# Pinning the weight-block sums of the feed-forward's second product to their place in program order

## The chip, the core and the metric

The kernel runs on one core of a Trainium2 chip. The metric is the device time of one execution in microseconds. The engines are TensorE (PE; its weight loads are PEld), VectorE (DVE), ScalarE (ACT), GpSimd (POOL) and SyncE (SP), which issues nearly all DMAs. Each works through its own queue in order; semaphores join them.

## The reference, cut to what matters

A decoder block on 512 positions of width 2048, in float32. Every product is made as three passes of a split number (high and low part), so a slice of weights costs a ScalarE copy and a VectorE subtraction before TensorE can use it.

```python
h = rmsnorm(x, norm_mix_g)
z = h @ w_in                                   # q, k, v, forget gates, zu, zv
attn = forgetting_attention(q, k, v, log_f)    # 8 heads, causal, softmax
gm = chunked_spatial_gating(zu, zv, ...)       # gelu, layernorm, 128 x 128 mixing
x = x + concat(rmsnorm(attn), rmsnorm(gm)) @ w_out
h2 = rmsnorm(x, norm_ffn_g)
a = relu(h2 @ w_ff1)                           # 2048 -> 8192
x = x + (a * a) @ w_ff2                        # 8192 -> 2048
out = rmsnorm(x, norm_final_g)
```

## The kernel before, in words

*Units and slices.* All products up to `w_ff1` are a list of units: `v0`, `qk0`, `qk1`, `v1`, `qk2`, `qk3`, `zv0`, `zv1`, `zu0`, `zu1` (16 weight slices each), eight units of the output projection (`oa`, `og`, 8 slices each) and `f0` to `f15`, the first feed-forward product (16 each): 160 + 64 + 256 = 480 slices. `run_units` walks them. For each slice it prepares the one three ahead (`load_pair`, L171, brings two slices in one DMA into one of four `raw` buffers; `split_w` makes `wh` on ScalarE, L162 or L158, and `wl` on VectorE, L163 or L159; there are four buffers of each), then issues 12 matmuls (L150 to L152), then at a unit's end its evacuation (`qk_done`, L335 and L338, for q and k), and then calls `tick()`.

*Tasks.* `tick()` advances every running task whose count of slices has run down; what a task issues then stands in program order at that slice. Attention is such a task: `head_task` issues the scores of one query block per slice (`pS`, one PSUM tile that all query blocks share), their maxima on VectorE (L380, L382), the exponential (L389), transposes (`pT`, L397), and the split of these (`ptl`, L400). So are the norms (`rB`, L146) and the gating (`u`, L532; its 128 x 128 weights `ws` come by GpSimd's queue, and L478 splits them).

*The sums.* The second feed-forward product uses seven block products instead of eight, which need sums of blocks of `w_ff2`. `sums_task` (L648) makes them ahead of time, in 64 rounds: load three blocks b12, b11, b22 (L655), two slices later add b12 to b11 and to b22 on VectorE (L657, L658), two slices later store both sums to DRAM (`t1d`, `t3d`, L660, L661), and three slices later the next round. `b_pool` has one buffer for each of the three. It starts 18 slices in. The second product (`second_product`, matmuls at L959) loads `t1d` and `t3d` again; it begins after the last slice.

*What sets the order.* Only TensorE's order is written by hand (`manual_schedule(engines={PE})`). On the other engines a scheduler orders the instructions when the kernel is built, by the time at which it takes each to be ready; an instruction whose inputs are early can so stand far ahead of its place in the program.

Of the kernel before, what the change touches and what calls it, by code (L numbers as in the profile page):

```python
# [12 lines left out]
ALU = mybir.AluOpType  # L13
# [21 lines left out]
def hybrid_block(ctx, tc, xT, win, wf_in, wout, w1, w2, cols_in, ln_in, ws_in, out):  # L35
    nc = tc.nc
# [608 lines left out]
    t1d = [dram.tile([2, P, 1024], F32, name=f"t1d{u}") for u in range(NU)]  # L645
    t3d = [dram.tile([2, P, 1024], F32, name=f"t3d{u}") for u in range(NU)]

    def sums_task():  # L648
        for u in range(NU):
            for n in range(2):  # L650
                for e in range(2):
                    c = slice(512 * e, 512 * (e + 1))
                    b11, b12, b22 = (b_pool.tile([P, 512], F32, tag=f"b{i}", name=f"b{u}{n}{e}{i}") for i in range(3))
                    for b, i in ((b12, 2), (b11, 0), (b22, 3)):
                        nc.sync.dma_start(out=b, in_=w2[8 * u + 4 * n + i][:, c])  # L655
                    yield 2
                    nc.vector.tensor_tensor(b11, b11, b12, ALU.add)  # L657
                    nc.vector.tensor_tensor(b22, b22, b12, ALU.add)  # L658
                    yield 2
                    nc.sync.dma_start(out=t1d[u][n][:, c], in_=b11)  # L660
                    nc.sync.dma_start(out=t3d[u][n][:, c], in_=b22)  # L661
                    yield 3

    mid = {}
# [355 lines left out]
    for u in range(NU):  # L1020
        f1_unit(u)
    start_task(attention_task())
    start_task(sums_task(), 18)
    run_units()
    for _ in mid["second"]:
# [51 lines left out]
```

## Time and profile before

| | us |
|---|---|
| median of 3 runs (2092.02 to 2095.45) | 2093.39 |
| the profiled execution | 2093.68 |
| its span, first to last instruction | 2090.8 |
| TensorE busy | 2029.5 (97%) |
| VectorE busy | 1268.1 (61%) |
| ScalarE busy | 903.3 (43%) |
| GpSimd busy | 225.6 (11%) |

By stage: to about 600 us run the ten units of the input projection with attention and gating beside them; to 727 us the output projection; to 1456 us the first feed-forward product; to 2053 us the second; then the last norm and the store. "Busy" counts the time in which an engine has at least one instruction under way. A wait is written "engine, line, waited for", with the total, the number of times and the longest; "[5.46 <-DMA b]" behind an instruction is the time that its engine stood idle before it, and what ended that.

### The profile page before, as it was taken

What the parts mean: (1) busy time and instruction counts of PE and PEld (TensorE: products, weight loads), DVE (VectorE), ACT (ScalarE), POOL (GpSimd) and SP (SyncE); (2) the same over time, 40 slices, a digit from 0 to 9 for tenths busy, and PEclk for the clock granted to TensorE, in tenths of its full rate; (3) what the DMA queues carried; (4) which work ended last, traced back from release to release, by engine and by line L of the source; (5) the groups of instructions that cost most, each with busy time, mean ns of one, the idle gap of its engine ahead of it and who ended that gap; (6) DMA issues with size and microseconds to landing.
All of it is one profiled execution on the core that took longest, in us unless ns stands there. A gap on an engine that the chain in (4) does not pass through costs nothing.

```text
span 2090.8 us, 24810 instructions
## 1 busy us (share of the span) xinstructions
PE 2029.5 (97%) x8992; PEld 1661.7 (79%) x8992; DVE 1268.1 (61%) x1769; ACT 903.3 (43%) x1424; POOL 225.6 (11%) x179
## 2 busy tenths in 40 slices
PE   9998998899999999999999999999999999999997
PEld 6777776778778888888888888888888888888886
DVE  7566566558676463344333443334767777777787
ACT  6233333435534243344333443335544444444455
POOL 4000001000042421121111211112000000000000
PEclk9999999999999999999999999999999999999999
DMA  6676676775763336545544455446777566666652
GB/s 238 226 241 225 224 242 214 225 230 172 229 205 112 120 121 222 221 171 199 199 166 171 171 201 200 163 171 262 270 283 262 188 245 252 215 228 241 240 203 81
DMA packets 152906, 431.13 MB, mean 206 GB/s; under 512 B 16080, under 2 KB 28496, under 8 KB 152656
## 3 DMA queue, kind: packets, MB, share of 16 engines
q1 hardware_dynamic: 152096, 427.69, 58.3%
q8 instruction: 70, 1.15, 0.2%
q10 hardware_dynamic: 432, 1.35, 0.2%
q0 software_dynamic: 256, 0.52, 0.1%
q14 instruction: 52, 0.43, 0.1%
HBM read 328.83 MB, written 100.66 MB: 205 GB/s over the span
## 4 chain that ended last, share of the span: by engine, by line
PE 72%; DMA 15%; DVE 8%; issue 3%; ACT 1%; SPq 0%; POOL 0%; DVEq 0%; POOLq 0%; ACTq 0%
PE bX L959 16%; PE ps_f L150 11%; PE ps_f L152 11%; PE ps_f L151 11%; DMA b<-in_w_dram 10%; PE bZ L959 8%; PE bY L959 4%; DMA t1d<-b 2%; DMA t3d<-b 2%; DVE b L658 1%; PE ps_og L152 1%; PE ps_og L151 1%; PE ps_og L150 1%; PE ps_oa L152 1%; PE ps_oa L150 1%
## 5 line engine op out<-in xcount | busy, mean ns | idle before, releaser
L159 DVE TENSOR_TENSOR wl_f<-raw_f,wh_f 128x512 fp32r<-128x512 f32 x256 | 193.7, 757 | 368.5 <-ACT wh_f L158 313.7
L150 PE MATMUL ps_f<-xh,wh_f 128*128 128x512 f32 x1024 | 398.9, 390 | 0.0
L152 PE MATMUL ps_f<-xh,wl_f 128*128 128x512 f32 x1024 | 398.5, 389 | 0.0
L151 PE MATMUL ps_f<-xl,wh_f 128*128 128x512 f32 x1024 | 398.4, 389 | 0.0
L787 DVE TENSOR_TENSOR wl<-raw,wh 128x1024 fp32r<-128x1024 f32 x224 | 273.8, 1227 | 135.4 <-ACT wh L786 133.6
L786 ACT CAST wh<-raw 128x1024 fp32r<-128x1024 f32 x224 | 236.2, 1054 | 262.5 <-PE bX L959 133.2
L959 PE MATMUL bX<-wh,fac 128*128 128x512 f32 x1008 | 319.9, 391 | 0.0
L158 ACT CAST wh_f<-raw_f 128x512 fp32r<-128x512 f32 x256 | 159.4, 623 | 330.9 <-PE ps_f L151 321.6
L959 PEld LDWEIGHTS bX<-wh,fac 128*128 128x128 f32 x1008 | 189.2, 188 | 46.9 <-ACT k L809 7.5
L152 PEld LDWEIGHTS ps_f<-xh,wl_f 128*128 128x128 f32 x1024 | 192.2, 188 | 40.0
L151 PEld LDWEIGHTS ps_f<-xl,wh_f 128*128 128x128 f32 x1024 | 192.2, 188 | 39.8
L150 PEld LDWEIGHTS ps_f<-xh,wh_f 128*128 128x128 f32 x1024 | 192.2, 188 | 39.8
L959 PE MATMUL bX<-wl,fac 128*128 128x512 f32 x504 | 196.3, 390 | 0.0
L959 PE MATMUL bZ<-wh,fac 128*128 128x512 f32 x512 | 162.8, 389 | 0.0
L657 DVE TENSOR_TENSOR b<-b,b 128x512 f32<-128x512 f32 x64 | 47.9, 749 | 131.6 <-DMA b<-in_w_dram 131.4
L959 PEld LDWEIGHTS bZ<-wh,fac 128*128 128x128 f32 x512 | 96.1, 188 | 19.9
L150 PE MATMUL ps_qk<-xh,wh_qk 128*128 128x512 f32 x256 | 103.7, 405 | 6.0 <-DVE qkt L335 5.7
L959 PEld LDWEIGHTS bX<-wl,fac 128*128 128x128 f32 x504 | 94.6, 188 | 18.7
L152 PE MATMUL ps_qk<-xh,wl_qk 128*128 128x512 f32 x256 | 101.2, 395 | 0.0
L151 PE MATMUL ps_qk<-xl,wh_qk 128*128 128x512 f32 x256 | 101.1, 395 | 0.0
L959 PE MATMUL bZ<-wl,fac 128*128 128x512 f32 x256 | 99.6, 389 | 0.0
L162 ACT ACTIVATE wh_qk<-raw_qk,cols 128x512 fp32r<-128x512 f32 x64 | 46.1, 722 | 87.9 <-PE ps_qk L151 64.2
(277 smaller groups left out, 3328.1 us busy)
## 6 DMA issues: line engine op xcount, KB each, us to landing
raw_f<-in_w_dram SPq DMA_DIRECT2D x128, 512.0 KB, 3.3
fac<-fc SPq DMA_DIRECT2D x112, 512.0 KB, 3.4
fac<-fac SPq DMA_DIRECT2D x112, 512.0 KB, 6.0
b<-in_w_dram SPq DMA_DIRECT2D x192, 256.0 KB, 4.3
raw<-in_w_dram SPq DMA_DIRECT2D x96, 512.0 KB, 5.0
raw_qk<-in_win_dram SPq DMA_DIRECT2D x32, 512.0 KB, 4.3
t1d<-b SPq DMA_DIRECT2D x64, 256.0 KB, 2.5
t3d<-b SPq DMA_DIRECT2D x64, 256.0 KB, 2.5
```

Of the source, the lines that this page charges most:

```text
L150: nc.tensor.matmul(ps, lhsT=ah, rhs=bh, start=start, stop=False)
L151: nc.tensor.matmul(ps, lhsT=ah, rhs=bl, start=False, stop=False)
L152: nc.tensor.matmul(ps, lhsT=al, rhs=bh, start=False, stop=stop)
L158: nc.scalar.copy(wh, raw)
L159: nc.vector.tensor_tensor(wl, raw, f(wh), ALU.subtract)
L162: nc.scalar.activation(wh, raw, AF.Copy, scale=g)
L657: nc.vector.tensor_tensor(b11, b11, b12, ALU.add)
L658: nc.vector.tensor_tensor(b22, b22, b12, ALU.add)
L786: nc.scalar.copy(wh, s)
L787: nc.vector.tensor_tensor(wl, s, f(wh), ALU.subtract)
L959: nc.tensor.matmul(banks[chain][t], lhsT=l, rhs=r, start=start and w == 0, stop=stop and w == 2, skip_group_check=True)
```

## The change

The three loads, two additions and two stores of each round are wrapped in `keep_in_program_order`. It ties an instruction behind the last one that was issued on its engine before it in program order, so the scheduler can't move it ahead of that one. It adds no instruction and no wait on a semaphore; other instructions may still move ahead of the tied ones.

```diff
+    here = tc.keep_in_program_order
+
     def sums_task():
...
                     for b, i in ((b12, 2), (b11, 0), (b22, 3)):
-                        nc.sync.dma_start(out=b, in_=w2[8 * u + 4 * n + i][:, c])
+                        here(nc.sync.dma_start(out=b, in_=w2[8 * u + 4 * n + i][:, c]))
                     yield 2
-                    nc.vector.tensor_tensor(b11, b11, b12, ALU.add)
-                    nc.vector.tensor_tensor(b22, b22, b12, ALU.add)
+                    here(nc.vector.tensor_tensor(b11, b11, b12, ALU.add))
+                    here(nc.vector.tensor_tensor(b22, b22, b12, ALU.add))
                     yield 2
-                    nc.sync.dma_start(out=t1d[u][n][:, c], in_=b11)
-                    nc.sync.dma_start(out=t3d[u][n][:, c], in_=b22)
+                    here(nc.sync.dma_start(out=t1d[u][n][:, c], in_=b11))
+                    here(nc.sync.dma_start(out=t3d[u][n][:, c], in_=b22))
                     yield 3
```

Two lines are inserted above, so behind L647 every line of the changed kernel counts two more: the loads are L657, the sums L659 and L660, the stores L662 and L663. TensorE's and GpSimd's orders are the same in both. Three places of the others, first before, then after:

VectorE in the first 100 us, between the splits of `qk` slices 3 and 4; `vl` is the evacuation of `v0`, `zf`, `dup` belong to the forget gates, `rB` is the norm row that they wait for, `b` are the sums. Before:

```order
L256 SCALAR_TENSOR_TENSOR vl_616<-ps_v_3_267,r_161,vh_615 128x512
L163 SCALAR_TENSOR_TENSOR wl_qk_3_667<-raw_qk_2_597,cols,wh_qk_3_666 128x512
L657 TENSOR_TENSOR b_1216<-b_1216,b_1217 128x512
L658 TENSOR_TENSOR b_1218<-b_1218,b_1217 128x512
L291 COPY zf<-pz 128x512
L296 COPY dup<-ident 64x8 x2
L297 TENSOR_TENSOR dup<-dup,ident 64x8 x2
L657 TENSOR_TENSOR b_1445<-b_1445,b_1446 128x512
L146 COPY rB<-pb_mix 128x512
```

After, with the rows that follow:

```order
L256 SCALAR_TENSOR_TENSOR vl_616<-ps_v_3_267,r_161,vh_615 128x512
L163 SCALAR_TENSOR_TENSOR wl_qk_3_667<-raw_qk_2_597,cols,wh_qk_3_666 128x512
L291 COPY zf<-pz 128x512
L296 COPY dup<-ident 64x8 x2
L297 TENSOR_TENSOR dup<-dup,ident 64x8 x2
L146 COPY rB<-pb_mix 128x512
L163 SCALAR_TENSOR_TENSOR wl_qk_4_693<-raw_qk_4_690,cols,wh_qk_4_692 128x512
L163 SCALAR_TENSOR_TENSOR wl_qk_5_715<-raw_qk_4_690,cols,wh_qk_5_714 128x512
L163 SCALAR_TENSOR_TENSOR wl_qk_6_753<-raw_qk_6_750,cols,wh_qk_6_752 128x512
L302 TENSOR_TENSOR z<-pz_730,rB 128x512
L659 TENSOR_TENSOR b_708<-b_708,b_709 128x512
```

The sums of the fourth and fifth round stood there (with three rounds ahead of them); now none stands ahead of `rB`, and the first sum of all follows slice 6.

SP's queue at the same place of the program, at the weight loads (`raw_qk`) of slices 12 and 14 of `qk0` and of the next unit; `b` are the blocks, `t1d` and `t3d` the stores. Before:

```order
L655 DMA b_1446<-in_w_dram 128x512
L655 DMA b_1445<-in_w_dram 128x512
L655 DMA b_1447<-in_w_dram 128x512
L660 DMA t1d_194<-b_1445 128x512
L661 DMA t3d_210<-b_1447 128x512
L655 DMA b_1680<-in_w_dram 128x512
L171 DMA raw_qk_12_868<-in_win_dram 128x1024
L655 DMA b_1679<-in_w_dram 128x512
L655 DMA b_1681<-in_w_dram 128x512
L660 DMA t1d_194<-b_1679 128x512
L661 DMA t3d_210<-b_1681 128x512
L171 DMA raw_qk_14_904<-in_win_dram 128x1024
```

After:

```order
L171 DMA raw_qk_12_868<-in_win_dram 128x1024
L662 DMA t1d_193<-b_708 128x512
L663 DMA t3d_209<-b_710 128x512
L657 DMA b_863<-in_w_dram 128x512
L657 DMA b_862<-in_w_dram 128x512
L171 DMA raw_qk_14_904<-in_win_dram 128x1024
L657 DMA b_864<-in_w_dram 128x512
L171 DMA raw_qk_0_940<-in_win_dram 128x1024
L171 DMA raw_qk_2_974<-in_win_dram 128x1024
L171 DMA raw_qk_4_1036<-in_win_dram 128x1024
L662 DMA t1d_193<-b_862 128x512
L663 DMA t3d_209<-b_864 128x512
```

A round of five transfers stood at nearly every weight load; now four weight loads lie between the stores of the first round and those of the second.

VectorE inside the first feed-forward product, at the splits of slices 10 to 15 of one `f` unit. Before:

```order
L159 TENSOR_TENSOR wl_f_10_6685<-raw_f_10_6682,wh_f_10_6684 128x512
L159 TENSOR_TENSOR wl_f_11_6701<-raw_f_10_6682,wh_f_11_6700 128x512
L159 TENSOR_TENSOR wl_f_12_6725<-raw_f_12_6722,wh_f_12_6724 128x512
L159 TENSOR_TENSOR wl_f_13_6741<-raw_f_12_6722,wh_f_13_6740 128x512
L159 TENSOR_TENSOR wl_f_14_6761<-raw_f_14_6758,wh_f_14_6760 128x512
L159 TENSOR_TENSOR wl_f_15_6777<-raw_f_14_6758,wh_f_15_6776 128x512
```

After:

```order
L159 TENSOR_TENSOR wl_f_10_6685<-raw_f_10_6682,wh_f_10_6684 128x512
L159 TENSOR_TENSOR wl_f_11_6701<-raw_f_10_6682,wh_f_11_6700 128x512
L159 TENSOR_TENSOR wl_f_12_6725<-raw_f_12_6722,wh_f_12_6724 128x512
L159 TENSOR_TENSOR wl_f_13_6741<-raw_f_12_6722,wh_f_13_6740 128x512
L659 TENSOR_TENSOR b_6716<-b_6716,b_6717 128x512
L660 TENSOR_TENSOR b_6718<-b_6718,b_6717 128x512
L159 TENSOR_TENSOR wl_f_14_6761<-raw_f_14_6758,wh_f_14_6760 128x512
L159 TENSOR_TENSOR wl_f_15_6777<-raw_f_14_6758,wh_f_15_6776 128x512
```

No sum stood in this product before; now a pair stands in every seven slices of it.

## Rows read from the trace of the kernel before

**Rows 1.** Stages: length, busy (instructions) PE, PEld, DVE, ACT, POOL; clock, DMA share, GB/s.

```profile
30.00:110.00 80.00, 74.11 (x312) 58.07 (x311) 45.15 (x70) 28.63 (x44) 10.76 (x9) 0.96 0.66 215
110.00:600.00 490.00, 448.62 (x2011) 365.31 (x2009) 321.45 (x679) 192.09 (x359) 38.70 (x39) 0.98 0.69 223
727.30:1455.70 728.40, 728.32 (x3232) 602.81 (x3231) 312.86 (x397) 299.12 (x519) 100.88 (x69) 1.00 0.51 187
1515.80:1568.10 52.30, 52.30 (x230) 42.87 (x230) 36.44 (x36) 24.81 (x28) 0.00 (x0) 1.00 0.77 283
```

**Rows 2.** TensorE's waits, 30 to 605 us: total, times, longest.

```profile
PE pS L150 <- DVE mx L382: 19.2, 11, 3.5
PE pm L150 <- DVE u L532: 6.1, 3, 3.2
PE ps_qk L150 <- DVE qkt L335: 5.7, 2, 3.6
PE ps_zv L151 <- DVE wl_zv L163: 4.9, 1, 4.9
PE pT L397 <- DVE ptl L400: 4.7, 4, 1.7
PE pz L300 <- DVE rB L146: 4.1, 1, 4.1
```

**Rows 3.** VectorE's waits, 30 to 605 us.

```profile
DVE b L657 <- DMA b<-in_w_dram: 131.4, 44, 5.7
DVE b L658 <- DMA b<-in_w_dram: 20.6, 20, 2.1
DVE rs L390 <- ACT p L389: 13.0, 18, 1.0
```

**Rows 4.** The timeline at 75 us: start, duration, instruction, idle before it.

```profile
75.43 0.69 DVE L657 TENSOR_TENSOR b<-b,b 128x512 f32<-128x512 f32 x1 [5.46 <-DMA b<-in_w_dram]
76.04 0.68 DVE L146 COPY rB<-pb_mix 128x512 f32<-128x512 f32 x1
...
76.87 1.19 PE L300 MATMUL pz<-zf,dup 128*128 128x512 f32 x1 [4.06 <-DVE rB L146]
```

**Rows 5.** The page, part 4: the chain that ended last, by line.

```profile
PE bX L959 16%; PE ps_f L150 11%; PE ps_f L152 11%; PE ps_f L151 11%; DMA b<-in_w_dram 10%; PE bZ L959 8%; PE bY L959 4%; DMA t1d<-b 2%; DMA t3d<-b 2%; DVE b L658 1%; PE ps_og L152 1%; PE ps_og L151 1%; PE ps_og L150 1%; PE ps_oa L152 1%; PE ps_oa L150 1%
```

**Rows 6.** Short stretches, columns as in rows 1; the clock is third from last.

```profile
75.10:81.90 6.80, 5.03 (x10) 3.38 (x11) 5.40 (x9) 0.00 (x0) 0.00 (x0) 0.50 0.55 154
121.20:124.60 3.40, 3.39 (x15) 2.83 (x16) 3.37 (x6) 2.89 (x5) 0.00 (x0) 1.00 0.96 311
228.70:232.10 3.40, 3.40 (x10) 2.63 (x9) 2.53 (x9) 1.47 (x4) 0.00 (x0) 0.50 1.00 255
...
587.00:590.40 3.40, 3.28 (x8) 2.64 (x9) 2.88 (x7) 0.30 (x1) 0.00 (x0) 0.51 0.87 278
```

**Rows 7.** The chain in order of time: start, length, what; 24 dense matmuls.

```profile
1461.15 5.44 PE bY L959 x24
```

**Rows 8.** DMA issues by line: count, KB each, median us from issue to landing.

```profile
raw_f<-in_w_dram SPq DMA_DIRECT2D x128, 512.0 KB, 3.3
...
b<-in_w_dram SPq DMA_DIRECT2D x192, 256.0 KB, 4.3
...
t1d<-b SPq DMA_DIRECT2D x64, 256.0 KB, 2.5
```

**Rows 9.** The timeline at 364 us.

```profile
363.73 0.80 DVE L478 TENSOR_TENSOR wsl<-ws,wsh 128x128 fp32r<-128x128 f32 x1 [4.59 <-ACT wsh L477]
...
364.95 0.45 PE L150 MATMUL pS<-qkh 128*128 128x384 f32 x1 [3.51 <-DVE mx L382]
```

**Rows 10.** The page, part 5: the two splits of a slice; busy, mean ns of one.

```profile
L159 DVE TENSOR_TENSOR wl_f<-raw_f,wh_f 128x512 fp32r<-128x512 f32 x256 | 193.7, 757 | 368.5 <-ACT wh_f L158 313.7
...
L158 ACT CAST wh_f<-raw_f 128x512 fp32r<-128x512 f32 x256 | 159.4, 623 | 330.9 <-PE ps_f L151 321.6
```

**Rows 11.** Waits of all engines, 620 to 1455 us.

```profile
ACT wh_f L158 <- PE ps_f L151: 321.6, 171, 2.9
```

## The prediction

> **What bounds the kernel now.** I read the busy time by stage first. From 727 us on TensorE is busy for 728.32 of 728.40 us, so nothing that only moves work can shorten that stretch. Between 30 and 600 us it is busy for 74.11 of 80 us and 448.62 of 490 us, 47.3 us short, and the granted clock is 0.96 and 0.98 there instead of 1.00 [rows 1]. So all that can be won stands in the first 600 us.
>
> Next come TensorE's waits in that stretch. They add up to the same 47.3 us, and nearly every one ends on VectorE: softmax maxima (19.2 us), the gating product (6.1), the evacuation of q and k (5.7), a weight split (4.9), transposes (4.7), the norm row rB (4.1), and five smaller ones, 2.6 together [rows 2].
>
> Then, what VectorE itself was doing. It stood 131.4 + 20.6 = 152 us at the two weight-block sums, waiting for their blocks to land, up to 5.7 us at a time; every other wait is small beside it: 13.0 us in 18 pieces for the exponentials, none over 1.0 [rows 3]. One place shows the link. VectorE reaches L657 and idles 5.46 us for a block; right behind it in its queue stands the copy of rB, which needs nothing from that block; TensorE waits 4.06 us for rB [rows 4]. An engine that works in order and meets a sum whose data is still travelling holds up everything behind it. In the chain that ended last, the loads of b are 10% and the stores 2% + 2% of the span [rows 5]: the sums run one after the other through a single set of buffers, and for 600 us that loop leads the kernel.
>
> **What the gaps cost in clock.** Seven stretches have the granted clock at 0.50, each beginning at one of these gaps. Six are 3.4 us long and hold 10, 10, 10, 8, 9 and 8 matmuls, 55 in all, where an undisturbed 3.4 us holds 15 [rows 6]. That is 90 - 55 = 35 matmuls, at 5.44/24 = 0.227 us each [rows 7], 7.9 us. The seventh, 75.1 to 81.9 us, holds 10 where 30 fit: 20 x 0.227 = 4.5 us, of which 6.80 - 5.03 = 1.8 us is idle time already counted, so 2.8 us. Together 10.7 us. The whole loss before 600 us is 47.3 + 10.7 = 58.0 us.
>
> The Trainium skill (TensorE: Matmul & The Clock Gate, What's actually happening) says that the slow level is the resting state and that activity releases it. The traced gaps agree only partly: after the 3.6 us wait for the evacuation of q and k [rows 2], at 121 us, the clock stayed at 1.00 [rows 6], so I count the seven stretches seen, not one per gap.
>
> The skill (Perfetto Trace Analysis, Identifying the Most-Contended Engine) also holds matmul busy time a poor measure and wants the busy share of weight loads instead. By that share, 0.726 and 0.746 early against 0.828 where TensorE is dense [rows 1], the loss would be 80 x 0.102/0.828 + 490 x 0.082/0.828 = 58 us; taken over the whole span it would promise 17% in the dense stretch too, which its 0.227 us from one matmul to the next denies.
>
> **What the change does, part by part.** No arithmetic, byte or instruction is added; TensorE's and GpSimd's order stay as they were. What moves is 128 sums on VectorE and 320 transfers on SP's queue.
>
> *Sums on VectorE.* The task starts after 18 weight slices and has one round per 7 slices, 64 rounds; with 12 matmuls a slice takes 12 x 0.227 = 2.72 us when dense, so a round comes every 19 us instead of every 9. The order shows it: no sum stands before rB any more, and later one pair stands in every seven slices. In the order 29 rounds stay ahead of the feed-forward product and 35 fall into it, the dense stretch. A round's loads are issued right behind the stores of the round before, some five slices (13 us) ahead of its sums, against 4.3 us to landing [rows 8]; so the waits of 152 us should all but vanish, and the rounds that stay cost their own 2 x 0.69 us [rows 4].
>
> *What stays of the 58.0 us.* First, a gap that the sums don't make: at 365 us TensorE waits 3.51 us for a maximum, after VectorE stood 4.59 us at a gating weight [rows 9], which comes by GpSimd's queue; that weight keeps its place among its neighbours. It stays with its slow stretch: 3.5 + 5 x 0.227 = 4.6 us. Second, the five small waits, 2.6 us. Third, the rounds left on VectorE. Of 64 first sums 44 waited for a block [rows 3], so 20 didn't; I put the gaps beside those 20 at about 3 us, an estimate of the size of the five small waits in [rows 2], 0.15 us each; 29 rounds then cost 4.4 us. Fourth, one further slow stretch, 1.3 us (35/6 x 0.227). Sum: 4.6 + 2.6 + 4.4 + 1.3 = 12.9 us.
>
> *The dense stretch.* It takes up 35 rounds: 35 x 1.38 = 48 us of VectorE, busy there for 313 of 728 us. What hides it: the splits of a slice start as soon as one of four buffers comes free, three slices (8.2 us) before use, and take 0.62 + 0.76 us [rows 10], so 6.8 us are to spare against 1.38; ScalarE waits there for TensorE, 321.6 us in all, and TensorE for nobody [rows 1, 11]. If that cover were gone it would cost up to 48 us. DMA: a round moves five times 256 KB, 1.31 MB; 35 in 728 us add 63 GB/s to 187, 250 in all, and the second product runs at 283 GB/s with TensorE full [rows 1]. I take nothing, and 48 us as the far end.
>
> *SP's queue.* A store waits for its sum, and in order behind it stand the next blocks (which wait for the store to land, 2.5 us [rows 8]) and three or four weight loads. After the first stores the next weight load is for slice 14 of its unit, while the sums stand beside slice 6: eight slices, 21.8 us; the closest I find in the dense stretch is six, 16.3 us. Against that stand 1.4 us of sums, 2.5 of landing and 3.3 for the weights [rows 8]: 7.2 us. I take nothing here either.
>
> **Sum.** The profiled execution took 2093.68 us, 2.9 us more than its span; the median of the three runs is 2093.39, so I use the first as it is. 2093.7 - 58.0 + 12.9 = 2048.6, said as 2049.
>
> **Rivals.** *The attention chain holds the gaps itself.* Matrix products of scores come 2.72 us apart and share one PSUM tile; if softmax on VectorE is too slow for that without any sum in between, the 19.2 + 4.7 us of waits on maxima and transposes stay [rows 2], with their three slow stretches, 17 matmuls short, 3.9 us. Won would be 58.0 - 23.9 - 3.9 = 30.2, less the small 2.6 and about half of the rounds' 4.4: 25 us, giving 2069. Against it: VectorE is busy for 321 of 490 us there, sums included, and its own waits in that chain are 1 us or less [rows 3].
>
> *Slower: SP's queue starves the weights.* Pinned stores stand before weight loads in the dense stretch, where no slack was needed so far. If a store comes so late that the load behind it misses its slice, a round costs a landing, 3.3 us [rows 8]; 35 rounds make 116 us, less the 45 won: 2164. It decides the sign from 45/35 = 1.3 us per round on. Against it: the 16.3 against 7.2 us above; the order would have to slip by three slices. The Trainium skill (Perfetto Trace Analysis, DMA Optimizations) speaks on its side: it suggests one DMA-capable engine for inputs and another for outputs, and here both share SP, before and after; no row shows a weight split late for its load in the dense stretch.
>
> *Little happens.* The pins hold the order but the early gain is given back in the dense stretch, 1.3 us a round, or the gaps have causes that the sums only accompany: 2093. The 4.06 us behind one block speak against it.
>
> **How the numbers follow.** Forecast 0.74, held by attention 0.17, starved weights 0.05, little 0.04. The forecast's own ends are 2036 (everything won, 2093.7 - 58.0) and about 2056 (the 12.9 that stays half as much again); the second rival reaches to 2069. The range 2035 to 2070 holds both. Within 0.2% (4 us) a measurement here can't tell from no change. Faster by more: 0.74 + 0.17, 0.91; same 0.03; slower 0.06, most of it starved weights.
>
> **What would show it.** Right: VectorE's wait for b under 10 us in all; TensorE's idle time before 600 us at some 12 us, the largest piece the gating weight's; at most two stretches at half clock there; sums spread to about 1,350 us; TensorE still full, at some 250 GB/s, from the first feed-forward product on. Wrong: waits on maxima as long as before with no sum beside them (the first rival), or TensorE waiting for splits after 700 us, with SP's loads held by stores (the second).

## The result, and the profile after

The changed kernel took 2031.43 us, the median of 4 runs (2029.58 to 2031.70), beside 2094.01 for the kernel before (4 runs, 2092.02 to 2095.45): a ratio of 0.970, interval 0.9683 to 0.9717. A second set of runs gave 2031.11, ratio 0.9697 (0.968 to 0.9715). The forecast was 2049 with a range from 2035 to 2070. Its sign and its mechanism hold; the time lies 4 us below the range, so the gain was put too small, 45 us for 62. The rest of this part reads the profiled execution of 2031.65 us, whose span is 2029.9.

First the stages, as in [rows 1]: length, busy time of PE, PEld, DVE, ACT and POOL with their instructions, then clock, DMA share and GB/s. The stages start earlier now; 675 us is where 727 was. The first matmul of `f0` itself starts at 755.4 us in the kernel before, not at 727 as the list of stages has it, and at 694.7 us in the changed one, so both stretches open with the end of the output projection. The last row is one short stretch, read below.

```profile
30.00:110.00 80.00, 78.97 (x349) 64.11 (x348) 43.52 (x67) 32.69 (x50) 10.76 (x9) 1.00 0.38 128
110.00:575.00 465.00, 462.01 (x2139) 383.69 (x2139) 296.28 (x635) 202.42 (x377) 52.34 (x50) 1.00 0.45 149
575.00:675.00 100.00, 100.00 (x458) 82.72 (x457) 72.30 (x81) 41.20 (x64) 37.53 (x24) 1.00 0.52 174
675.00:1396.00 721.00, 720.92 (x3200) 596.79 (x3199) 349.69 (x461) 295.25 (x514) 101.17 (x70) 1.00 0.71 253
329.70:333.10 3.40, 3.40 (x10) 2.83 (x9) 2.28 (x10) 1.40 (x4) 1.29 (x3) 0.50 0.09 28
```

TensorE now lacks 1.0 us of the first 80 and 3.0 of the next 465, and the clock is at full speed in both. The dense stretch has taken the other rounds (253 GB/s for 187) and TensorE is still busy for all of it. VectorE works no less: 349.69 of 721 us there, where [rows 1] had 313 of 728.

TensorE's waits between 30 and 605 us, all of them (total, times, longest), where [rows 2] had 47.3 us:

```profile
PE pS L150 <- DVE mx L382: 3.0, 1, 3.0
PE ps_v L151 <- DVE wl_v L163: 0.8, 1, 0.8
PE ps_v L150 <- ACT wh_v L162: 0.2, 1, 0.2
```

Next, the view of the tile `b`. Its rows give minimum, median and maximum of one operation in ns and its first and last start; the last two lines are the idle time ahead of the sums, with its count:

```profile
L659 DVE TENSOR_TENSOR b<-b,b x64: 673/686/1809, 73.0 to 1341.6; 128x512 f32<-128x512 f32 x64
...
its engine sat idle before it (us, times) until:
  DMA b<-in_w_dram: 1.5, 2
```

The 152 us of VectorE's waits for blocks [rows 3] are 1.5 us, and a sum still takes 0.69 us. Before, the same view has the first sums from 40.2 to 609.8 us, one round every 569.6/63 = 9.0 us; now it is one every 1268.6/63 = 20.1 us.

The one gap left is the gating weight's, 35 us earlier than in [rows 9] and smaller. The timeline at 328 us (start, duration, instruction, idle before it and what ended that):

```profile
328.19 0.80 DVE L478 TENSOR_TENSOR wsl<-ws,wsh 128x128 fp32r<-128x128 f32 x1 [1.48 <-ACT wsh L477]
...
329.41 0.41 PE L150 MATMUL pS<-qkh 128*128 128x384 f32 x1 [2.99 <-DVE mx L382]
```

Right behind it lies the only stretch at half clock (1.2 instead of 2.4 GHz), the last row of the stages: 10 matmuls in 3.40 us where 15 fit, as in [rows 6].

The page's chain that ended last, by engine and by line, where [rows 5] had the loads of `b` at 10%:

```profile
PE 96%; DVE 2%; issue 1%; DMA 1%; ACT 0%; POOL 0%; SPq 0%; POOLq 0%; DVEq 0%
PE bX L961 17%; PE ps_f L150 11%; PE ps_f L152 11%; PE ps_f L151 11%; PE bZ L961 8%; PE bY L961 4%; PE ps_qk L150 3%; PE ps_qk L152 3%; PE ps_qk L151 3%; PE ps_oa L152 1%; PE ps_oa L150 1%; PE ps_zu L152 1%; PE ps_oa L151 1%; PE ps_zu L151 1%; PE ps_zu L150 1%; PE ps_zv L150 1%
```

No transfer of `b` is left in that line; the chain is TensorE's own work. The transfers themselves became slower, not faster, as the last number (median us to landing) shows beside [rows 8]:

```profile
raw_f<-in_w_dram SPq DMA_DIRECT2D x128, 512.0 KB, 4.8
...
b<-in_w_dram SPq DMA_DIRECT2D x192, 256.0 KB, 4.5
t1d<-b SPq DMA_DIRECT2D x64, 256.0 KB, 3.1
```

It costs TensorE nothing, though ScalarE now waits a little for weights, which it didn't before. From 620 to 1395 us:

```profile
ACT wh_f L158 <- DMA raw_f<-in_w_dram: 15.3, 5, 4.3
```

### The profile page after: what moved, and what is told of

The parts are those of the page before. It is cut to its first block, busy times and chain, and to the rows that moved or that the text cites. A ratio compares the mean times of both kernels' runs of the same rounds, so it can differ in the third digit from the quotient of the medians.

```text
span 2029.9 us, 24801 instructions
## 1 busy us (share of the span) xinstructions
PE 2011.3 (99%) x8992; PEld 1656.5 (82%) x8992; DVE 1273.8 (63%) x1769; ACT 904.1 (45%) x1424; POOL 226.3 (11%) x179
## 4 chain that ended last, share of the span: by engine, by line
PE 96%; DVE 2%; issue 1%; DMA 1%; ACT 0%; POOL 0%; SPq 0%; POOLq 0%; DVEq 0%
PE bX L961 17%; PE ps_f L150 11%; PE ps_f L152 11%; PE ps_f L151 11%; PE bZ L961 8%; PE bY L961 4%; PE ps_qk L150 3%; PE ps_qk L152 3%; PE ps_qk L151 3%; PE ps_oa L152 1%; PE ps_oa L150 1%; PE ps_zu L152 1%; PE ps_oa L151 1%; PE ps_zu L151 1%; PE ps_zu L150 1%; PE ps_zv L150 1%
## 5 line engine op out<-in xcount | busy, mean ns | idle before, releaser
L158 ACT CAST wh_f<-raw_f 128x512 fp32r<-128x512 f32 x256 | 159.3, 623 | 319.2 <-PE ps_f L151 285.8
L163 DVE SCALAR_TENSOR_TENSOR wl_qk<-raw_qk,cols,wh_qk 128x512 fp32r<-128x512 f32 x64 | 47.8, 749 | 64.1 <-ACT wh_qk L162 63.7
```

What stands on the lines that cost most here:

```text
L158: nc.scalar.copy(wh, raw)
L163: nc.vector.scalar_tensor_tensor(wl, raw, g, f(wh), ALU.mult, ALU.subtract)
```

## The experiments

The theory: VectorE, working in order, stood at sums whose blocks were still travelling, and TensorE waited for what stood behind them. The rivals: it was the DMA traffic of the early rounds, or the sums' own 1.4 us a round, or attention. All times are medians; edits are shown against the changed kernel, and none leaves any of the computation out.

### Which of the pins does it

Only the two sums pinned, loads and stores left to the scheduler:

```diff
-                        here(nc.sync.dma_start(out=b, in_=w2[8 * u + 4 * n + i][:, c]))
+                        nc.sync.dma_start(out=b, in_=w2[8 * u + 4 * n + i][:, c])
...
-                    here(nc.sync.dma_start(out=t1d[u][n][:, c], in_=b11))
-                    here(nc.sync.dma_start(out=t3d[u][n][:, c], in_=b22))
+                    nc.sync.dma_start(out=t1d[u][n][:, c], in_=b11)
+                    nc.sync.dma_start(out=t3d[u][n][:, c], in_=b22)
```

> Only the two sums of a round are pinned; loads and stores float as before the change. Waiting theory (VectorE no longer meets a sum whose block still travels): the sums stand where they stand in the changed kernel, so the whole gain stays: 2031 us, within 3 us; VectorE's wait for b under 5 us. If SP's order makes the gain, most of it goes: 2060 us or more.

2032.28 us, ratio 0.9697 (0.9676 to 0.9718): the whole gain. The sums run from 72.5 to 1341.4 us and VectorE waits 1.5 us for blocks, as in the changed kernel. The 128 pins on VectorE are enough; a store can't go ahead of its sum, nor a load ahead of the store that frees its buffer, so the transfers follow.

The other half, only the transfers pinned:

```diff
-                    here(nc.vector.tensor_tensor(b11, b11, b12, ALU.add))
-                    here(nc.vector.tensor_tensor(b22, b22, b12, ALU.add))
+                    nc.vector.tensor_tensor(b11, b11, b12, ALU.add)
+                    nc.vector.tensor_tensor(b22, b22, b12, ALU.add)
```

> Only loads and stores are pinned; the sums float, and in the order they stand up to seven slices ahead of their place in the changed kernel. Waiting theory: where the order takes a block to have landed sooner than it does, VectorE waits again; some 20 to 60 us of waits for b in all, 2033 to 2050 us. If SP's order makes the gain: 2031 us and no waits.

2034.44 us, 0.9706 (0.9682 to 0.9731): nearly all of it again. Either half holds the pace; the scheduler, left free with the sums, only puts them a little too early. VectorE's waits at the first sum of a pair, from 30 to 605 us and from 675 to 1395:

```profile
DVE b L659 <- DMA b<-in_w_dram: 27.6, 16, 4.2
```

```profile
DVE b L659 <- DMA b<-in_w_dram: 73.8, 32, 5.7
```

And its dense stretch, columns as in the stages above:

```profile
675.00:1396.00 721.00, 719.95 (x3195) 595.70 (x3194) 347.62 (x456) 295.09 (x513) 101.22 (x69) 1.00 0.71 250
```

Here is a point that the theory in its short form misses. VectorE stands for 73.8 us at sums and TensorE loses 1 us. A stall at a sum is a loss only where what stands behind it is wanted at once; in the dense stretch splits are made some slices ahead. Early on, 27.6 us in 16 waits left TensorE's waits between 30 and 1395 us at 5.3 us in all. The many waits of before, 152 us with a round every 9 us, did use up the slack.

### Was it the traffic?

Traffic without waits put back into the first 600 us: 128 copies of 256 KB from DRAM to DRAM, on SP's queue.

```diff
+    spare = [dram.tile([P, 512], F32, name=f"spare{i}") for i in range(4)]
+
+    def traffic_task():
+        for r in range(64):
+            for j in range(2):
+                here(nc.sync.dma_start(out=spare[2 * (r % 2) + j], in_=w2[2 * r + j][:, 0:512]))
+            yield 3
...
+    start_task(traffic_task(), 12)
```

> The changed kernel with 128 copies of 256 KB from DRAM to DRAM, two in every three slices over the first 200 slices, pinned on SP's queue: about 33 MB, so that the first 600 us move about as much as before the change (223 GB/s against 149). Nothing waits for them, no sum moves. Waiting theory: 2031 to 2035 us. Traffic theory (weights and blocks land sooner because less is moved beside them): half of the gain or more is lost, 2060 us or more.

2034.90 us, 0.9709 (0.9677 to 0.9741). Its stage from 110 to 575 us:

```profile
110.00:575.00 465.00, 459.94 (x2125) 381.89 (x2124) 295.04 (x634) 201.74 (x376) 52.36 (x50) 0.99 0.60 202
```

At 202 GB/s, against 223 before [rows 1] and 149 after the change, TensorE lacks 5.1 us of 465, and all of it is one wait, the gating weight's, which grew from 3.0 to 5.1 us. So 53 of the 74 GB/s came back, as copies that stay in DRAM, for 3.5 us by the medians or 1.9 by the ratios, whose intervals overlap. The traffic isn't what held TensorE.

### Putting the waits back

The loads of a round issued at the sums' own slice, on ScalarE's queue:

```diff
                     for b, i in ((b12, 2), (b11, 0), (b22, 3)):
-                        here(nc.sync.dma_start(out=b, in_=w2[8 * u + 4 * n + i][:, c]))
-                    yield 2
+                        here(nc.scalar.dma_start(out=b, in_=w2[8 * u + 4 * n + i][:, c]))
...
-                    yield 3
+                    yield 5
```

> The changed kernel with the three loads of a round issued by ScalarE's queue and the sums pinned at the same slice as the loads, one round per seven slices as in the changed kernel: the sums' place and the traffic are those of the changed kernel, but VectorE meets each sum before its blocks have landed, some 4 us each. Waiting theory: about 27 early rounds x 4 us = 100 us of waits, of which TensorE takes over about a third with its slow clock, 2055 to 2080 us; from the first feed-forward product on the 6.8 us to spare hide them. Traffic theory, and the theory that VectorE just has less to add early: 2031 us.

2036.81 us, 0.9718 (0.9684 to 0.9752). As a test of the early waits this failed: the pin ties a sum to what stands before it, but other instructions may still go ahead of it, and the scheduler let them. Early on only 6.4 + 4.7 us of waits came back. In the dense stretch 46.0 + 45.1 us did, and TensorE was busy there for 720.89 of 721 us. That second part says the same as the experiment before: in the dense stretch such waits are covered.

So the pace was changed instead, everything left pinned on SP and VectorE. Four slices a round, then three, then two:

```diff
-                    yield 2
+                    yield 1
                     here(nc.vector.tensor_tensor(b11, b11, b12, ALU.add))
                     here(nc.vector.tensor_tensor(b22, b22, b12, ALU.add))
                     yield 2
...
-                    yield 3
+                    yield 1
```

> The changed kernel with a round per four slices instead of seven (sums one slice after the loads, next loads one slice after the stores): 43 rounds in the first 600 us instead of 25, still pinned. A round needs some 9 us, four slices give 11 to 13. Waiting theory: no waits for b to speak of, 2031 to 2036 us. Load theory (VectorE and the DMA queues just have less to do early): 43 of 62 rounds are back where they were, so (43 - 25)/(62 - 25), about half of the gain, is lost: 2060 us.

2030.01 us, 0.9694 (0.9666 to 0.9722). The sums now end at 823 us, 12.0 us a round, and 50 of the 64 rounds have their first sum before 675 us (28 in the changed kernel), at 194 GB/s from 110 to 575 us; TensorE waits 2.4 us between 30 and 605 us, less than in the changed kernel. Rounds that don't wait cost the early part nothing that can be seen.

```diff
-                    yield 2
+                    yield 1
...
-                    yield 2
+                    yield 1
...
-                    yield 3
+                    yield 1
```

> A round per three slices, pinned: 57 rounds in the first 600 us, nearly as many as before the change (62), with the same traffic and the same additions. Three slices give 8.2 us where dense and 9.8 with attention beside them, against 9 for a round. Waiting theory: waits return where slices are dense, 20 to 60 us in all, 2033 to 2055 us. Load theory: nearly all of the gain is lost, 2085 us.

2044.61 us, 0.9764 (0.9736 to 0.9792). VectorE's waits, 30 to 700 us:

```profile
DVE b L659 <- DMA b<-in_w_dram: 45.0, 23, 4.7
...
DVE b L660 <- DMA b<-in_w_dram: 9.9, 12, 2.0
```

The waits are back, TensorE lacks 670 - 658.34 = 11.7 us of that stretch (its waits in the changed kernel were 4.0), and the time is 13.2 us above the changed kernel's.

```diff
-                    yield 2
+                    yield 1
...
-                    yield 2
+                    yield 1
...
-                    yield 3
```

> A round per two slices, pinned: faster than its own loop of load, sum and store can turn. In the order the 64 rounds stand between slices 21 and 159. Waiting theory: the loop leads the kernel, 64 rounds x 9 us = 576 us for 138 slices that take 450 us by themselves: 2130 to 2170 us, slower than before the change, with over 150 us of VectorE waits for b. Load theory: as before the change, 2090 us.

2113.03 us, 1.0091 (1.0061 to 1.012): 0.9% slower than before, with every instruction of the rounds pinned, though less so than the 2130 to 2170 that I had put down. VectorE's waits from 30 to 700 us, and the stage that lost most:

```profile
DVE b L659 <- DMA b<-in_w_dram: 127.6, 58, 5.7
DVE b L660 <- DMA b<-in_w_dram: 31.9, 33, 4.9
```

```profile
110.00:575.00 465.00, 404.56 (x1773) 325.07 (x1774) 289.74 (x637) 167.20 (x314) 27.79 (x31) 0.96 0.72 234
```

So much for the pins as such. The place that the program gives to a round has to leave it the time for its loop, and the pin then holds it there.

### A stall of VectorE with no sum and no transfer

To see what a stall alone does, one copy in attention (`nFm`, once per head) is made nine times over, eight of them for nothing:

```diff
-        nc.vector.tensor_tensor(nFm.rearrange("p (t c) -> p t c", c=P), pB.rearrange("p (t c) -> p t c", c=P),
-                                mask.unsqueeze(1).broadcast_to([P, NT, P]), ALU.add)
+        for _ in range(9):
+            tc.keep_in_program_order(nc.vector.tensor_tensor(
+                nFm.rearrange("p (t c) -> p t c", c=P), pB.rearrange("p (t c) -> p t c", c=P),
+                mask.unsqueeze(1).broadcast_to([P, NT, P]), ALU.add))
```

> The changed kernel with the row of masked gates nFm computed nine times instead of once for each head (same result): 8 x 0.68 = 5.4 us of VectorE more at each of 8 heads, 43 us in all, none of it waiting. What a gap on TensorE costs: TensorE's recorded idle time grows by 15 to 30 us in some 8 to 16 waits. My account: the time grows by that idle time, by 0.16 us for each wait (the record runs to the modelled end of a matmul, 0.39 us, while the next could start after 0.227) and by 1.3 to 1.8 us for each stretch at half clock. Rival account (the one in the forecast): idle time and the slow stretches alone.

2092.15 us, 0.9985 (0.9973 to 0.9996): the whole gain is gone, by chance to within 0.2%, without one wait for a block. TensorE's waits, 30 to 605 us, and the stage:

```profile
PE pO L150 <- DVE nFm L368: 34.7, 6, 8.7
PE pS L150 <- DVE mx L384: 11.8, 2, 6.4
```

```profile
110.00:575.00 465.00, 418.45 (x1865) 346.27 (x1865) 300.73 (x643) 181.61 (x340) 27.81 (x33) 0.94 0.39 129
```

Eight waits make 46.5 us; with the two small ones TensorE's waits are 47.5 us, 43.5 more than after the change, and the time is 60.7 us longer. That settles two things. A stall of VectorE reaches TensorE with no wait for a transfer in it, at 129 GB/s. And a microsecond that TensorE waits cost about 1.4 in time here; most of what is over shows as clock, 0.94 in this stage.

### The gap that was left

The split of the gating weight pinned as well:

```diff
-        nc.scalar.copy(wsh, ws)
-        nc.vector.tensor_tensor(wsl, ws, f(wsh), ALU.subtract)
+        tc.keep_in_program_order(nc.scalar.copy(wsh, ws))
+        tc.keep_in_program_order(nc.vector.tensor_tensor(wsl, ws, f(wsh), ALU.subtract))
```

> The changed kernel with the split of the gating weights (L477 and L478) pinned to its place too. Waiting theory: the last gap, 3.0 us and its stretch at half clock (five matmuls short, 1.1 us), goes the same way as those of the sums: 2027 us. If that gap has another cause than the order: 2031 us.

2026.93 us (2026.59 to 2028.08), 0.9677 (0.9662 to 0.9693). None of its runs reaches into those of the changed kernel beside it (2029.74 to 2031.63). TensorE's waits between 30 and 605 us are the two small ones alone, and from 110 to 575 us it is busy for all of it:

```profile
110.00:575.00 465.00, 465.00 (x2161) 386.39 (x2160) 298.89 (x638) 204.03 (x379) 53.96 (x50) 1.00 0.46 152
```

It is the fastest of all versions, 4.2 us below the changed kernel and 3.2% below the one before. The same edit with four slices a round besides:

```diff
-        nc.scalar.copy(wsh, ws)
-        nc.vector.tensor_tensor(wsl, ws, f(wsh), ALU.subtract)
+        tc.keep_in_program_order(nc.scalar.copy(wsh, ws))
+        tc.keep_in_program_order(nc.vector.tensor_tensor(wsl, ws, f(wsh), ALU.subtract))
...
-                    yield 2
+                    yield 1
                     here(nc.vector.tensor_tensor(b11, b11, b12, ALU.add))
                     here(nc.vector.tensor_tensor(b22, b22, b12, ALU.add))
                     yield 2
...
-                    yield 3
+                    yield 1
```

> The gating weights pinned and a round per four slices. Waiting theory: neither costs anything, 2027 to 2029 us, no wait of TensorE over 1 us between 30 and 700 us.

2028.36 us (2027.92 to 2029.09), 0.9684 (0.9666 to 0.9701). With the gating gap closed the pace of four adds nothing; by its rows the gaps are the same two small ones.

### How much the dense stretch can take

The other end: no round at all before slice 230, and then one per three slices, so that all 64 fall into the dense stretch.

```diff
-                    yield 2
+                    yield 1
...
-                    yield 2
+                    yield 1
...
-                    yield 3
+                    yield 1
...
-    start_task(sums_task(), 18)
+    start_task(sums_task(), 230)
```

> The changed kernel with the sums started at slice 230, one round per three slices: none stands in the first 600 us, all 64 in the first feed-forward product. Waiting theory: what the 25 rounds of the first 600 us cost by themselves is nothing, so 2031 us less the gap at the gating weight if that moves, 2027 to 2032; TensorE stays full in the feed-forward product in spite of twice the rounds. If the rounds that stayed did cost the 4.4 us of the forecast: 2026 us with the gap still there. If weights starve behind stores: over 2040 us.

2082.69 us, 0.9937 (0.9922 to 0.9953). 51 of the 62 us are lost again, in another place. Two stages of it:

```profile
25.00:590.00 565.00, 563.95 (x2598) 467.05 (x2597) 330.87 (x675) 247.87 (x448) 70.89 (x64) 1.00 0.26 89
700.00:1000.00 300.00, 289.10 (x1254) 236.62 (x1253) 151.74 (x207) 108.77 (x194) 36.98 (x26) 0.98 0.88 301
```

Without rounds the first part is as good as full (1.1 us short of 565), and the gating gap is gone too. The dense stretch is no longer full. Waits of all engines there, from 700 to 1400 us, and SP's queue in the same stretch:

```profile
ACT wh_f L158 <- DMA raw_f<-in_w_dram: 172.7, 30, 13.5
...
DVE b L659 <- DMA b<-in_w_dram: 90.2, 32, 7.5
...
PE ps_f L150 <- ACT wh_f L158: 32.1, 11, 4.6
```

```profile
SPq L662 <- DVE b L659: 184.3, 63, 5.6
...
SPq L657 <- DMA t1d<-b: 64.2, 59, 3.3
```

This is the second rival of the prediction, seen for the first time: SP stands at stores that wait for their sums and at loads that wait for a store to land, the weight loads stand behind them, and TensorE waits for the split. The chain of waits at 800 us (start, length, what) shows one full turn of the loop that SP is held by:

```profile
798.61 4.39 DMA b<-in_w_dram
...
803.82 0.61 DVE b L660
...
804.45 3.59 DMA t3d<-b
...
808.10 4.77 DMA b<-in_w_dram
```

Load, sum, store, load again: 808.10 - 798.61 = 9.5 us, in a kernel that gives a round three slices, 3 x 2.73 = 8.2 us. Either the loop is too long or the DMA is too busy, at 301 GB/s. Two more runs tell these apart; the first also puts the rounds' five transfers on GpSimd's queue.

```diff
-                        here(nc.sync.dma_start(out=b, in_=w2[8 * u + 4 * n + i][:, c]))
-                    yield 2
+                        here(nc.gpsimd.dma_start(out=b, in_=w2[8 * u + 4 * n + i][:, c]))
+                    yield 1
...
-                    here(nc.sync.dma_start(out=t1d[u][n][:, c], in_=b11))
-                    here(nc.sync.dma_start(out=t3d[u][n][:, c], in_=b22))
-                    yield 3
+                    here(nc.gpsimd.dma_start(out=t1d[u][n][:, c], in_=b11))
+                    here(nc.gpsimd.dma_start(out=t3d[u][n][:, c], in_=b22))
+                    yield 1
...
+    start_task(sums_task(), 230)
```

> The late sums at a round per three slices (2083 us, ScalarE waiting 173 us for weights), but with the five transfers of a round issued by GpSimd's queue, so that no weight load stands behind a store. If SP's order starves the weights: the loss goes, 2027 to 2035 us. If the DMA engines do (301 GB/s in that stretch): it stays, 2070 us or more.

2193.70 us, 1.0471 (1.044 to 1.0501), 111 us worse than on SP's queue. Waits from 700 to 1450 us:

```profile
DVE b L659 <- DMA b<-in_w_dram: 327.2, 60, 9.1
...
PE ps_f L152 <- DVE wl_f L159: 102.7, 49, 5.8
```

The weights are free: ScalarE's wait for `raw_f`, 172.7 us on SP's queue, isn't there at all. But a block takes 5.9 us to land instead of 4.5, an issue occupies the queue for 0.55 us instead of 0.33, a round takes 681/63 = 10.8 us, and now it is VectorE, standing at the sums for 383 us, that holds the splits back. GpSimd's queue cures the weights and lengthens the loop, and the loop decides. Which part of the longer loop comes from issuing, landing or GpSimd's own work isn't settled. Nor is this a test of any other queue: the page of this run lists the rounds' transfers as `software_dynamic`, those of SP as `hardware_dynamic`.

The second keeps SP's queue and gives a round four slices, 10.9 us, from slice 210 on:

```diff
-                    yield 2
+                    yield 1
                     here(nc.vector.tensor_tensor(b11, b11, b12, ALU.add))
                     here(nc.vector.tensor_tensor(b22, b22, b12, ALU.add))
                     yield 2
...
-                    yield 3
+                    yield 1
...
-    start_task(sums_task(), 18)
+    start_task(sums_task(), 210)
```

> The sums started at slice 210, a round per four slices, transfers on SP's queue: all 64 rounds in the first feed-forward product, a quarter fewer per slice than at three. A round of load, sum, store and landing needs some 9 us, four slices give 10.9, three gave 8.2. If what starves the weights at three is SP waiting for a round that can't turn in time: 2027 to 2032 us. If it is the DMA rate, which falls to about 290 GB/s: most of the loss stays, 2060 us or more.

2032.00 us, 0.9699 (0.9669 to 0.9728): the full gain again, with all rounds in the last stages.

```profile
700.00:1000.00 300.00, 298.24 (x1326) 246.32 (x1325) 151.20 (x210) 116.12 (x207) 37.15 (x26) 1.00 0.90 311
1000.00:1300.00 300.00, 300.00 (x1325) 248.51 (x1324) 156.48 (x214) 121.30 (x215) 40.84 (x28) 1.00 0.86 304
```

More bytes per second than at three slices, 311 and 304 GB/s, and TensorE is short of 1.8 us in 600. So the rate of the DMA alone didn't break the pace of three; a round was asked for sooner than it could turn. The rate may still have a part in how long that takes: the rounds of two slices turned in 8.2 us beside 234 GB/s, these of three in 9.5 beside 301, and no run separates the two. ScalarE waits for weights here too, from 700 to 1400 us, and it costs next to nothing, so the 172.7 us above aren't by themselves the loss either:

```profile
ACT wh_f L158 <- DMA raw_f<-in_w_dram: 111.7, 27, 9.3
```

### All of them by the time of a round

The view of `b` gives the first and the last of the first sums; their distance over 63 is the time of a round. VectorE's waits for `b` are of the same view. TensorE's idle time is of 30 to 605 us (before, after and four slices), 30 to 700 (three and two), 30 to 1396 (all late ones but GpSimd's, which is 700 to 1400).

| kernel | slices per round | us per round | VectorE waits for `b` | TensorE idle | time |
|---|---|---|---|---|---|
| two slices, pinned, early | 2 | 8.2 | 159.5 | 62.2 | 2113.0 |
| before, not pinned | - | 9.0 | 152.3 | 47.3 | 2094.0 |
| three slices, pinned, early | 3 | 9.4 | 55.0 | 11.7 | 2044.6 |
| three slices, late | 3 | 9.5 | 96.9 | 33.3 | 2082.7 |
| three slices, late, GpSimd's queue | 3 | 10.8 | 383.1 | 106.1 | 2193.7 |
| four slices, late | 4 | 11.0 | 64.8 | 2.9 | 2032.0 |
| four slices, early | 4 | 12.0 | 19.2 | 2.4 | 2030.0 |
| the changed kernel | 7 | 20.1 | 1.5 | 4.0 | 2031.4 |

Wherever rounds follow one another as closely as 8.2 to 9.5 us on SP's queue, or 10.8 on GpSimd's, VectorE or SP stands at them and TensorE follows. From 11 us a round on, on SP's queue, the three medians lie within 2 us of one another, whether the rounds lie early, late or across.

## Why the prediction was right, and where it was too small

*The bound and the link: right.* TensorE's idle time before 600 us went from 47.3 to 4.0 us when VectorE's waits for blocks went from 152 to 1.5. Most of the traffic put back cost 2 to 3.5 us, which the intervals can't tell from nothing; a stall of VectorE without traffic cost 60.7.

*The sums on VectorE: right.* Rounds every 19 us were forecast, 20.1 measured; sums to 1350 us, measured 1342; waits for `b` under 10 us, measured 1.5.

*The dense stretch and SP's queue: right at this pace.* 250 GB/s were forecast, 253 measured, with TensorE at 720.92 of 721 us, and ScalarE's wait for TensorE is only down from 321.6 us [rows 11] to 285.8. The Trainium skill (Perfetto Trace Analysis, Optimization Strategy) suggests interleaving regimes whose busiest engines differ; the trace agrees here, since 36 of the 64 rounds have their first sum after 675 us now, beside a TensorE that lacks 0.1 us of 721. Some of the margin of 16.3 against 7.2 us was used, as ScalarE's 15.3 us of waits for weights suggest; at three slices a round, with another order of SP's queue, none was left.

*The first rival is out.* Waits on maxima fell from 19.2 to 3.0 us and those on transposes from 4.7 to none, with no change to attention. *The second is real but not at this pace*: at three slices a round SP's queue did starve the weights, for 51 us and not 116. The rule of the Trainium skill that spoke on its side (Perfetto Trace Analysis, DMA Optimizations: separate engines for inputs and outputs) wasn't tried in that form; GpSimd's queue for the rounds, in both directions, made the time longer by 111 us. *Little happens* is out.

**Two steps failed: "what stays of the 58.0 us" was put too large, and the 58.0 us that could be won, the sum of "what the gaps cost in clock", too small.** The first has four terms, forecast and measured, from the profiled executions:

| what stays | forecast | measured |
|---|---|---|
| the gating weight's gap and its slow stretch | 4.6 | 3.0 + 1.1 = 4.1 |
| small waits | 2.6 | 1.0 |
| the rounds left on VectorE | 4.4 | 0 |
| one further slow stretch | 1.3 | 0 |
| sum | 12.9 | 5.1 |

The third was the guess of 0.15 us beside each round that doesn't wait. The runs leave nothing of it: no gap at all remains that a sum ends, at four slices a round TensorE waits 2.4 us over even more early rounds, and with the gating weight pinned only the two small waits are left, early rounds or not. A sum of 0.69 us whose data has landed is covered by what TensorE has in hand. This makes 7.8 of the 16.9 us that were missed (62.0 won in the profiled executions, 2093.68 to 2031.65, for 45.1 forecast).

**The 58.0 is the second.** I had added up idle time as the rows give it and slow stretches by their matmuls. Another count is from one matmul's start to the next; no view gives it, it is made from the start times in the trace. It takes all of the some 3,100 matmuls from the first of slice 0 (before 30 us) to the first of `f0`, and takes off the median of each shape at full clock, 675.4 us in all in either kernel. Number of starts in brackets:

| excess over the undisturbed spacing | before | after | less |
|---|---|---|---|
| starts that follow a wait | 54.2 (35) | 6.7 (7) | 47.5 |
| starts at half clock | 12.3 (59) | 1.5 (8) | 10.8 |
| all others | 7.0 | 4.7 | 2.3 |

The recorded idle time fell by 43.3 and the slow clock by 10.7 - 1.1 = 9.6, 52.9 together. By starts it is 47.5 + 10.8 + 2.3 = 60.6, 7.7 more. The largest part is in the waits: a dense matmul is recorded as 0.39 us long but starts every 0.227, so at each wait some 0.39 - 0.227 = 0.16 us of lost time is shown as busy. In the 35 waits before, 48.1 us are recorded as idle and 54.2 lost, 0.17 us more for each; 28 gaps fewer, 35 to 7, make 28 x 0.16 = 4.5 us, and 47.5 - 43.3 = 4.2 are found. The other 3.5 us are smaller disturbances at slow clock and elsewhere, of which no row shows a cause. Around the span 2.9 us became 1.75, 1.1 more; the other fourteen profiled executions lie between 1.7 and 2.1 there, further executions of the kernel before between 1.7 and 3.2, and why some have more stays open. That leaves 0.3 us.

So the 17 us are 7.8 of idle and slow time that I left standing, 7.7 that my sum of idle time and slow stretches didn't hold, and 1.4 of rest. The range failed for the second reason: its lower end of 2035 rested on 58.0 as the most that could be won, and 58.0 was no upper bound. The stall put into attention can't decide between the two counts: its waits are few and long, so that they differ by some 1 us there.

## What to carry to other kernels

Where a background task shares an in-order engine with the critical path, the place of its instructions has to leave it time for its whole loop (here load, sum, store, about 9 us through single buffers); here a scheduler that took a sum to be ready early put it where the engine stood for it. Pinning is only as good as the place: the same pins made 2030 us at four slices a round and 2113 at two. And the idle time that the trace recorded was less here than what removing it won: count starts as well, and let the range go beyond the sum of the gaps.

## What the runs showed that I had not expected

- TensorE's recorded idle time is short by about 0.16 us for each wait, because a dense matmul's recorded length (0.39 us) is longer than the distance between starts (0.227 us).
- A stall of VectorE at data under way can be free: 73.8 us of it beside a TensorE that was busy for 719.95 of 721 us, and 58.9 us in the late run at four slices a round. So can one of ScalarE at weights, 111.7 us in that same run.
- TensorE stays all but full (298.24 of 300 us) beside 311 GB/s of DMA, more than the 283 of the second product [rows 1]; the same rounds asked for a little sooner starve it at 301.
- On GpSimd's queue the same transfers took 0.55 us to issue for 0.33, and a block 5.9 us to land for 4.5.
- The half clock follows only some gaps. After the change, the one gap of 3.0 us was followed by 3.4 us at 0.50; behind the 1.4 us gap at four slices a round it stayed at 1.00 (the row below, columns as above), and so it did behind the 3.6 us wait before the change [rows 2, 6].

```profile
331.60:335.00 3.40, 3.32 (x15) 2.76 (x16) 2.46 (x9) 1.47 (x4) 0.29 (x1) 1.00 0.44 159
```
